# Layer 4's last twelve pairs of feature-major units with a Strassen scheme: seven products of quarters in place of eight

## Chip, cores and metric
One core of one Trainium2 chip. The time is device microseconds of one launch, the median of repeated runs. TensorE (PE in the profile) does the matrix products, VectorE (DVE) and ScalarE (ACT) the element work, SyncE (SP) issues the weight transfers. "PEld" is TensorE's loading of the stationary operand.

## What is computed
Two blocks of two layers each, in float32, on 512 tokens of 2048 features. Only layer 4 is touched by the change:

```python
u, v, z = jnp.split(h @ w_in, 3, axis=-1)          # h: 512 x 2048, w_in: 2048 x 6144
u = jax.nn.gelu(u)
v = layer_norm(jax.nn.gelu(v), ln_g, ln_b)
v = v.reshape(b, s // 128, 128, 8, 256)
mixed = jnp.einsum('gts,bnsgc->bntgc', w_s, v) + b_s.T[None, None, :, :, None]
y = u * mixed.reshape(b, s, 2048) * jax.nn.silu(z)
return y @ w_out
```

## The kernel before
Every product keeps float32 accuracy by splitting both operands into a high and a low part: `mm3` issues three matmuls (high x high, high x low, low x high) where a plain product has one. The layer's operand stands in SBUF as `Ah` and `Al`, 16 blocks of 128 features ("k blocks"), each 512 tokens wide. A weight chunk of 128 x 1024 is loaded into a `raw` tile by SP (`w_load`), copied to its high part `h` by ACT (`w_high`, L150) and subtracted to its low part `l` by DVE (`w_low`, L156); `w_get` keeps the preparation two chunks ahead of the chunk that it hands out, with four `h` and four `l` buffers and three `raw` buffers.

The program is unrolled by hand: each engine executes its own instructions in the order in which the code writes them. Element work that goes beside the products is written as generators in `self.side`; `pump`, called after every fourth k block of a unit (12 matmuls), lets each of them write its next piece. So the place of a piece among the matmuls is a count of pumps. `run_until` pumps with no matmul between until a condition holds.

Layer 4 first computes v, token-major, in four items (`tm_item`). Then 16 pairs of feature-major units (`fm_unit`): one of 128 features of u, one of 128 features of z, each 16 k blocks x 3 matmuls of 512 columns into one PSUM bank, two weight chunks. Beside the first units runs the generator `spatial` (from L1515): sums of squares on ACT; a layer norm on DVE (L1548 and L1549, 16 pairs of instructions, and some small ones for each of four token tiles; a `yield` after each pair); then 18 steps, each with the split of one column block of v (ACT cast L174, DVE subtraction L175), twelve small matmuls of 128 columns for the block split one pump before, and the bias addition L1556 for the one before that. Gelu of u is L1576, its product with the mixed v L1579; the tanh, sum and product for z are L937, L938 and L1589. After the 16 pairs the out projection (`out_proj`) begins: it multiplies with 512 columns (`fg_item`) and at its end with 256 (`fg_last`).

Of the kernel before, what the change touches and what calls it, by code (L numbers as in the profile page):

```python
# [6 lines left out]
F32 = mybir.dt.float32  # L7
# [3 lines left out]
ALU = mybir.AluOpType  # L11
# [5 lines left out]
KC = 16  # L17
# [10 lines left out]
SCH_END = ["", "S", "", "P", "c", "c", "c", "c"]  # L28


class Core:
# [76 lines left out]
    def w_ahead(self, n, dma=0):  # L108
        n = min(n, len(self.wlist))
        while self.wprep < n or self.wdma < dma:  # L110
            while self.wdma < max(dma, min(self.wprep + 3, len(self.wlist)) if self.wprep < n else 0):
# [17 lines left out]

    def w_load(self):  # L130
        raw = self.p_raw.tile([128, 1024], F32, tag="raw", name="raw")
        src = self.wlist[self.wdma]
        n = src.shape[1]
# [8 lines left out]
    def w_high(self):  # L142
        if self.wpend or self.wprep >= len(self.wlist):
            return
        while self.wdma < min(self.wprep + 3, len(self.wlist)):
            self.w_load()
        raw, n = self.wraw.pop(self.wprep)
# [19 lines left out]
    def mm3(self, out, lh, ll, rh, rl, start, stop):  # L167
        mm = self.nc.tensor.matmul
        mm(out=out, lhsT=lh, rhs=rh, start=start, stop=False)  # L169
        mm(out=out, lhsT=lh, rhs=rl, start=False, stop=False)  # L170
        mm(out=out, lhsT=ll, rhs=rh, start=False, stop=stop)  # L171
# [116 lines left out]
    def fg_last(self, kperm, bd):  # L288
        """The last two units, token half by token half."""
# [64 lines left out]
    # -- start: x from the input; 1/rms is applied to the first layer's products  # L354
# [67 lines left out]
    # during a layer's last products: the mix that is done takes the place of operands that nothing reads any more  # L422
# [15 lines left out]
    # -- out projection of a layer, feature by feature: B gets x_new * gain, xd[i] the residual stream  # L438
# [189 lines left out]
    # ---------------- layer 1  # L628
# [7 lines left out]
    def layer1(self):  # L636
# [25 lines left out]
        # log sigmoid of lambda, times 4, and half biases  # L662
# [311 lines left out]
    # ---------------- layer 2  # L974
# [307 lines left out]
    # ---------------- modulation rows  # L1282
# [57 lines left out]
    # ---------------- layer 3  # L1340
# [150 lines left out]
    # ---------------- layer 4  # L1491
    def plan4(self):
        a = self.a
        w = [a["w4t"][j, c] for j in range(4) for c in range(8)]
        w += [a["w4f"][u, c] for u in range(32) for c in range(2)]
        w += [a["wo4"][j, c] for j in range(4) for c in range(8)]
        return w

    def layer4(self):
# [3 lines left out]
        done = {}  # L1503
# [11 lines left out]
        def spatial():  # L1515
# [27 lines left out]
            for t in range(NT):  # L1543
                s = sums[t]
                r = self.rms_tile(s[:, 8:12])
                for j in range(4):
# [3 lines left out]
                    yield  # L1550
            X, P = {}, {}
            for i in range(KC + 2):
                if i >= 2:
# [4 lines left out]
                    done["s", m] = True  # L1558
                if 1 <= i <= KC:
# [38 lines left out]
        for n in range(KC):  # L1598
            self.fm_unit(evac_u(n))
            if n == KC - 1:  # L1600
                self.mix_early(list(range(KC)), lambda k: k in mix_done)
            self.fm_unit(evac_z(n))
        return list(range(KC)), lambda k: k in mix_done

    # ---------------- whole
    def run(self):
        L = self.layers
        plans = {1: self.plan1, 2: self.plan2, 3: self.plan3, 4: self.plan4}
        for l in L:
            self.wlist += plans[l]()  # L1610
# [49 lines left out]
def fm(w):  # L1660
    U = w.shape[1] // 128
    w = w.reshape(2, 8, 128, U, 128)
    return np.ascontiguousarray(w.transpose(3, 0, 2, 1, 4)).reshape(U, 2, 128, 1024)

# [16 lines left out]
def layout(inp):  # L1681
# [36 lines left out]
    # layer 2  # L1718
# [15 lines left out]
    # layer 3  # L1734
# [16 lines left out]
    # layer 4  # L1751
# [5 lines left out]
    d["w4f"] = fm(w[:, np.concatenate(order)])  # L1757
# [25 lines left out]
```

## Time and profile before
| what | value |
|---|---|
| median of three runs | 3379.75 us (3377.02 to 3380.16) |
| profiled execution, first to last instruction (its span, the only time listed of it) | 3376.1 us |
| TensorE busy | 3354.3 us, 99% of the span |
| VectorE, ScalarE busy | 1894.8 us (56%), 1223.4 us (36%) |
| TensorE's share of the chain that ended last | 99% |

The span leaves out what lies around the instructions, 3.65 us against the median. Busy shares are means over stages; layer 4 runs from about 2630 to the end, its 16 pairs of units from about 2802 to 3170.

### The profile page before, as it was taken

The numbers are of one execution on the slowest core, as the hardware profiler recorded it, in microseconds if no ns is written. First come the engines' busy times: TensorE is split into PE (matmuls) and PEld (weight loads), VectorE is DVE, ScalarE is ACT, GpSimd is POOL, SyncE is SP. The second block draws the span as 40 slices with busy tenths as digits, with TensorE's granted clock in tenths as the row PEclk, the third lists the DMA queues.
The fourth block names the chain that finished last, engine by engine and source line by source line (L and its number), as shares of the span: only waits on it lengthen the run. The fifth ranks groups of instructions, "written<-read, shape, count | busy, mean of one in ns | idle before, by whom it ended". The sixth has DMA issues, their size and how long they took to land.

```text
span 3376.1 us, 40334 instructions
## 1 busy us (share of the span) xinstructions
PE 3354.3 (99%) x15596; PEld 2766.4 (82%) x15596; DVE 1894.8 (56%) x3179; ACT 1223.4 (36%) x1966; POOL 113.5 (3%) x208
## 2 busy tenths in 40 slices
PE   9999999999999999999999999999999999999998
PEld 7888888888888888888888888888888888888887
DVE  7766676568656566564576665544434526533334
ACT  5355553343333233344542322322333424222332
POOL 0000000100000000001000000000000000000000
PEclk9999999999999999999999999999999999999999
DMA  5422235645454445444344444322333422223232
GB/s 207 153 81 81 76 103 182 202 133 173 153 162 152 157 153 179 136 156 145 123 141 156 149 161 171 109 88 88 112 125 129 144 96 88 97 97 107 95 107 92
DMA packets 155088, 443.92 MB, mean 131 GB/s; under 512 B 19429, under 2 KB 19557, under 8 KB 154896
## 3 DMA queue, kind: packets, MB, share of 16 engines
q1 hardware_dynamic: 140832, 398.95, 35.5%
q0 software_dynamic: 14064, 42.40, 4.0%
q8 instruction: 122, 2.00, 0.2%
q14 instruction: 70, 0.57, 0.1%
HBM read 424.36 MB, written 16.91 MB: 131 GB/s over the span
## 4 chain that ended last, share of the span: by engine, by line
PE 99%; DVE 0%; DMA 0%; ACT 0%; issue 0%; SPq 0%; DVEq 0%; ACTq 0%
PE ps L169 32%; PE ps L171 32%; PE ps L170 32%; PE ps L178 2%; DMA raw<-in_w1t 0%; PE ps L1310 0%; PE ps L1311 0%; PE ps L519 0%; DVE s L529 0%; PE ps L505 0%; DVE l L156 0%; SPq L366 0%; ACT h L150 0%; ACT B L484 0%; ACT s L479 0%
## 5 line engine op out<-in xcount | busy, mean ns | idle before, releaser
L169 PE MATMUL ps<-Ah,h 128*128 128x512 f32 (+1 forms) x3200 | 1240.2, 388 | 0.0
L171 PE MATMUL ps<-Ah,l 128*128 128x512 f32 (+1 forms) x3200 | 1230.1, 384 | 0.0
L170 PE MATMUL ps<-Al,h 128*128 128x512 f32 (+1 forms) x3200 | 1225.2, 383 | 0.0
L156 DVE TENSOR_TENSOR l<-raw,h 128x1024 fp32r<-128x1024 f32 (+2 forms) x559 | 675.0, 1209 | 735.4 <-ACT h L150 726.5
L150 ACT CAST h<-raw 128x1024 fp32r<-128x1024 f32 (+2 forms) x559 | 577.3, 1035 | 863.2 <-PE ps L170 503.0
L171 PEld LDWEIGHTS ps<-Ah,l 128*128 128x128 f32 x3200 | 601.7, 188 | 127.9
L170 PEld LDWEIGHTS ps<-Al,h 128*128 128x128 f32 x3200 | 602.1, 188 | 122.8 <-issue 0.2
L169 PEld LDWEIGHTS ps<-Ah,h 128*128 128x128 f32 x3200 | 602.3, 188 | 117.4 <-issue 0.2
L169 PE MATMUL ps<-h,Ah 128*128 128x512 f32 (+2 forms) x1408 | 547.9, 389 | 7.1 <-ACT h L174 5.8
L170 PE MATMUL ps<-l,Ah 128*128 128x512 f32 (+2 forms) x1408 | 543.9, 386 | 0.8 <-DVE l L156 0.8
L171 PE MATMUL ps<-h,Al 128*128 128x512 f32 (+2 forms) x1408 | 544.2, 386 | 0.4
L169 PEld LDWEIGHTS ps<-h,Ah 128*128 128x128 f32 x1408 | 265.5, 189 | 64.1 <-ACT h L174 5.8
L171 PEld LDWEIGHTS ps<-h,Al 128*128 128x128 f32 x1408 | 265.2, 188 | 60.9 <-DVE Al L551 1.6
L170 PEld LDWEIGHTS ps<-l,Ah 128*128 128x128 f32 x1408 | 265.4, 189 | 57.9 <-DVE l L156 1.1
L1301 DVE SCALAR_TENSOR_TENSOR s<-s,sc 128x512 f32<-128x512 f32 x360 | 268.8, 747 | 5.8 <-DMA s<-in_ab_wm 1.7
L175 DVE TENSOR_TENSOR s<-ps,s 128x512 fp32r<-128x512 f32 (+2 forms) x178 | 101.1, 569 | 153.8 <-ACT s L174 153.7
L174 ACT CAST s<-ps 128x512 fp32r<-128x512 f32 (+2 forms) x178 | 86.1, 491 | 242.9 <-PE ps L178 168.1
L169 PE MATMUL ps<-s 128*128 128x512 f32 (+2 forms) x384 | 131.6, 343 | 0.0
L171 PE MATMUL ps<-s 128*128 128x512 f32 (+2 forms) x384 | 129.5, 337 | 1.3 <-DVE s L175 1.3
L170 PE MATMUL ps<-s 128*128 128x512 f32 (+2 forms) x384 | 128.8, 335 | 0.0
L476 ACT ACTIVATE s<-s 128x512 f32<-128x512 f32 (+1 forms) x72 | 42.0, 583 | 136.3 <-DVE s L468 73.3
L171 PEld LDWEIGHTS ps<-s 128*128 128x128 f32 x384 | 72.5, 189 | 10.2 <-DVE s L175 1.5
(271 smaller groups left out, 2026.6 us busy)
## 6 DMA issues: line engine op xcount, KB each, us to landing
raw<-in_wo SPq DMA_DIRECT2D x128, 512.0 KB, 3.5
raw<-in_w3f SPq DMA_DIRECT2D x112, 512.0 KB, 3.5
s<-in_ab_wm SPq DMA_DIRECT2D x192, 256.0 KB, 4.2
s<-in_sg_wm SPq DMA_DIRECT2D x192, 256.0 KB, 4.1
raw<-in_w2t SPq DMA_DIRECT2D x88, 512.0 KB, 3.6
raw<-in_w4f SPq DMA_DIRECT2D x64, 512.0 KB, 3.5
raw<-in_w1f SPq DMA_DIRECT2D x48, 512.0 KB, 3.6
raw<-in_w2f SPq DMA_DIRECT2D x32, 512.0 KB, 3.6
```

Of the source, the lines that this page charges most:

```text
L150: self.nc.scalar.copy(out=h[:, 0:n], in_=raw[:, 0:n])
L156: self.nc.vector.tensor_tensor(out=l[:, 0:n], in0=raw[:, 0:n], in1=h[:, 0:n].bitcast(F32), op=ALU.subtract)
L169: mm(out=out, lhsT=lh, rhs=rh, start=start, stop=False)
L170: mm(out=out, lhsT=lh, rhs=rl, start=False, stop=False)
L171: mm(out=out, lhsT=ll, rhs=rh, start=False, stop=stop)
L174: self.nc.scalar.copy(out=h, in_=src)
L175: self.nc.vector.tensor_tensor(out=l, in0=src, in1=h.bitcast(F32), op=ALU.subtract)
L178: self.nc.tensor.transpose(out, src, self.idt)
L476: nc.scalar.activation(out=sq[0], in_=xn, func=AF.Square)
L1301: nc.vector.scalar_tensor_tensor(out=acc, in0=raw, scalar=ck, in1=acc, op0=ALU.mult, op1=ALU.add)
```

## The change
Of the 16 pairs of units in layer 4 the first `N4` = 4 stay as they are. The other 12 become `pair_unit`: u and z of a pair, times two token halves of 256, over k blocks 0 to 5 against 8 to 13 (`M4` = 6) are a 2 x 2 by 2 x 2 product of quarters, done with seven products instead of eight. The k blocks 6, 7, 14 and 15 are added in the ordinary way. Every matmul of a pair then has 256 columns: 7 products x 6 blocks x 3, and 2 features x 4 blocks x 2 halves x 3.

The weight sums are made on the fly: of eight chunks in a pair (seven of 768 columns, one of 1024) five are loaded and four are, or replace, a difference made on DVE in the `raw` tile before the split (`w.comb`, L193). The operand sums are made once: `pair_prep` makes three sums ("1", "2", "4") in three pieces of two k blocks each and keeps their high and low parts in 18 `s` tiles; `pair_last` overwrites the second token half of blocks 0 to 5 of `Ah` and `Al` with a difference ("3"). `pair_prep` is let into its first piece by the end of the layer norm, into its second when v's blocks 0 to 7 are mixed, into its third when all 16 are. Products that are needed twice are copied out of PSUM by ACT between the products (L338, L341, L344, L351, L380) and added on DVE (L352, L377 to L379); the next product but one of a pair goes into the same PSUM half. The layer norm yields after two pairs of instructions instead of one. The pool `raw` has 4 buffers instead of 3, the pool `s` 26 instead of 28.

```diff
-        self.p_raw = pool(name="raw", bufs=3)
+        self.p_raw = pool(name="raw", bufs=4)
-        self.p_s = pool(name="s", bufs=28)
+        self.p_s = pool(name="s", bufs=26)
...
+def pair_steps(q, r, m):
+    st = {}
+    n = m * 128
+    w = [Step(q[0], n, st, "a"), Step(q[1], n, st, "b", ("b", "b", "a")), Step(None, n, st, None, ("b", "c", "b")),
+         Step(None, n, st, "c"), Step(None, n, st, None, ("a", "b", "a")), Step(q[3], n, st, "d"),
+         Step(None, n, st, None, ("b", "d", "b"))]
+    w[2].src, w[2].key = q[2], "c"
+    w[6:6] = [Step(x, x.shape[1]) for x in r]
+    return w
...
+        if w.comb:
+            raw, x, y = (w.st[c] for c in w.comb)
+            self.nc.vector.tensor_tensor(out=raw[:, 0:n], in0=x[:, 0:n], in1=y[:, 0:n], op=ALU.subtract)
...
+    def pair_prep(self, m):
+        def raw(hf, k):
+            x = self.s()
+            tt(out=v(x), in0=q(self.Ah.bitcast(F32), hf, k), in1=q(self.Al.bitcast(F32), hf, k), op=ALU.add)
+            return x
+        def keep(nm, c, x):
+            h, l = self.sr(), self.sr()
+            self.split(h, l, x)
+            S[nm, c] = v(h), v(l)
+        for c in range(n):
+            while not self.pair_room(c):
+                yield
+            k = 2 * c
+            x21, x22 = raw(1, k), raw(1, 8 + k)
+            tt(out=x22, in0=x21, in1=x22, op=ALU.add)
+            yield
+            keep("1", c, x22)
+            x11 = raw(0, k)
+            tt(out=x22, in0=x22, in1=x11, op=ALU.subtract)
+            yield
+            keep("2", c, x22)
+            x12 = raw(0, 8 + k)
+            tt(out=x12, in0=x12, in1=x22, op=ALU.subtract)
+            yield
+            keep("4", c, x12)
...
+    def pair_last(self, m):
+        for c in range(m // 2):
+            k = 2 * c
+            x, y = self.s(), self.s()
+            for o, hf in ((x, 0), (y, 1)):
+                tt(out=v(o), in0=q(self.Ah.bitcast(F32), hf, k), in1=q(self.Al.bitcast(F32), hf, k), op=ALU.add)
+            tt(out=x, in0=x, in1=y, op=ALU.subtract)
+            self.split(q(self.Ah, 1, k), q(self.Al, 1, k), v(x))
+            yield
+        self.S["3"] = True
...
+    def pair_unit(self, m, evu, evv, early=()):
...
+        prod(x, A(lo, 0), True)
+        nc.scalar.copy(out=tu[:, lo], in_=x)
+        self.pump()
+        prod(y, S("1"), True)
+        nc.scalar.copy(out=t5[:, lo], in_=y)
+        self.pump()
+        prod(x, S("2"), False)
+        nc.scalar.copy(out=tv[:, lo], in_=x)
+        self.pump()
+        prod(y, S("4"), False)
+        self.pump()
+        if "3" not in self.S:
+            self.run_until(lambda: "3" in self.S)
+        prod(x, A(hi, 0), False)
+        nc.scalar.copy(out=tv[:, hi], in_=x)
+        nc.vector.tensor_tensor(out=tv[:, hi], in0=tv[:, hi], in1=t5[:, lo], op=ALU.add)
+        self.pump()
+        prod(w0, A(lo, 8), True)
...
+        prod(x, A(hi, 8), False)
...
@@ def layer4
-                    yield
+                    if j % 2:
+                        yield
+            done["ln"] = True
...
-        for n in range(KC):
+        self.pair_room = lambda c: ("ln" if c == 0 else ("sg", c - 1)) in done
+        self.S = None
+        self.add(self.pair_prep(M4))
+        for n in range(N4):
             self.fm_unit(evac_u(n))
-            self.fm_unit(evac_z(n))
+            self.fm_unit(evac_z(n))
+        self.run_until(lambda: self.S)
+        self.add(self.pair_last(M4))
+        for n in range(N4, KC):
...
+            self.pair_unit(M4, evac_u(n), evac_z(n), early)
```

How the instructions stand: first VectorE at the end of the layer norm, its last token tile. Before (L1548 and L1549 the norm, L156 the low part of a weight chunk, L175 the low part of v's first blocks):

```order
L1548 SCALAR_TENSOR_TENSOR B<-B,t,s 128x512
L1549 SCALAR_TENSOR_TENSOR B<-B,t,s 128x512
L156 TENSOR_TENSOR l<-raw,h 128x1024
L1548 SCALAR_TENSOR_TENSOR B<-B,t,s 128x512
L1549 SCALAR_TENSOR_TENSOR B<-B,t,s 128x512
L1548 SCALAR_TENSOR_TENSOR B<-B,t,s 128x512
L1549 SCALAR_TENSOR_TENSOR B<-B,t,s 128x512
L156 TENSOR_TENSOR l<-raw,h 128x1024
L1548 SCALAR_TENSOR_TENSOR B<-B,t,s 128x512
L1549 SCALAR_TENSOR_TENSOR B<-B,t,s 128x512
L175 TENSOR_TENSOR s<-B,s 128x512
```

and in the change (L1711 and L1712 the norm, L202 the weight chunk, L221 the low part of v's first block, L280 the first sums of `pair_prep`):

```order
L1711 SCALAR_TENSOR_TENSOR B<-B,t,s 128x512
L1712 SCALAR_TENSOR_TENSOR B<-B,t,s 128x512
L1711 SCALAR_TENSOR_TENSOR B<-B,t,s 128x512
L1712 SCALAR_TENSOR_TENSOR B<-B,t,s 128x512
L202 TENSOR_TENSOR l<-raw,h 128x1024
L1711 SCALAR_TENSOR_TENSOR B<-B,t,s 128x512
L1712 SCALAR_TENSOR_TENSOR B<-B,t,s 128x512
L1711 SCALAR_TENSOR_TENSOR B<-B,t,s 128x512
L1712 SCALAR_TENSOR_TENSOR B<-B,t,s 128x512
L221 TENSOR_TENSOR s<-B,s 128x512
L280 TENSOR_TENSOR s<-Ah,Al 128x512 x2
```

A token tile has one weight chunk among its norm instead of two. On TensorE the first small matmul of `spatial` stands behind 204 matmuls of the units instead of behind 300.

Second, VectorE in the change from the last bias additions of `spatial` (L1721), which stand at the start of the first pair's first product, on: the third piece of `pair_prep` (L280, L293, L297, L301 with the low parts L221), the z of unit 3 (L1099, L1756), the third weight chunk's difference and low part (L193, L202), and the first piece of `pair_last` (L315).

```order
L1721 TENSOR_TENSOR B<-ps,s 128x4x128 x2
L280 TENSOR_TENSOR s<-Ah,Al 128x512 x2
L293 TENSOR_TENSOR s<-s 128x512
L1099 SCALAR_TENSOR_TENSOR s<-s,ps 128x512
L1756 SCALAR_TENSOR_TENSOR B<-s,B 128x4x128
L221 TENSOR_TENSOR s<-s 128x512
L280 TENSOR_TENSOR s<-Ah,Al 128x512
L297 TENSOR_TENSOR s<-s 128x512
L221 TENSOR_TENSOR s<-s 128x512
L280 TENSOR_TENSOR s<-Ah,Al 128x512
L301 TENSOR_TENSOR s<-s 128x512
L221 TENSOR_TENSOR s<-s 128x512
```

None of this stands on VectorE before; there the units of pair 4 go on with one L156 in 24 matmuls. Third, ScalarE in the change over the same stretch (L220 the high parts, L196 the weights, L338 to L351 the copies out of PSUM):

```order
L220 CAST s<-s 128x512 x3
L196 CAST h<-raw 128x768
L338 COPY s<-ps 128x256
L220 CAST Ah<-s 128x2x256
L196 CAST h<-raw 128x768
L341 COPY s<-ps 128x256
L220 CAST Ah<-s 128x2x256
L196 CAST h<-raw 128x768
L344 COPY s<-ps 128x256
L220 CAST Ah<-s 128x2x256
L196 CAST h<-raw 128x768
L196 CAST h<-raw 128x1024
```

Each copy out of PSUM stands behind the cast of the weight chunk two products later.

## Rows read from the trace of the kernel before

**Rows 1.** The page: span, busy time of each engine, chain that ended last.
```profile
span 3376.1 us, 40334 instructions
...
PE 3354.3 (99%) x15596; PEld 2766.4 (82%) x15596; DVE 1894.8 (56%) x3179; ACT 1223.4 (36%) x1966; POOL 113.5 (3%) x208
...
PE 99%; DVE 0%; DMA 0%; ACT 0%; issue 0%; SPq 0%; DVEq 0%; ACTq 0%
```

**Rows 2.** Busy time by stretch: during the norm, and after `spatial`; columns in the first line.
```profile
core 0: us, PE busy (x) PEld busy (x) DVE busy (x) ACT busy (x) POOL busy (x), PEclk, DMA share, GB/s
...
2840.00:2852.00 12.00, 12.00 (x55) 9.82 (x54) 11.58 (x26) 2.63 (x4) 0.00 (x0) 1.00 0.26 87
...
2960.00:2972.00 12.00, 12.00 (x53) 9.70 (x52) 3.54 (x4) 2.58 (x3) 0.08 (x1) 1.00 0.34 110
```

**Rows 3.** Timeline of ScalarE: gelu of u (L1576), start us and us, 16 units apart.
```profile
2968.41 0.60 ACT L1576 ACTIVATE s<-ps 128x512 f32<-128x512 f32 x1 [4.78 <-PE ps L171]
...
3147.61 0.60 ACT L1576 ACTIVATE s<-ps 128x512 f32<-128x512 f32 x1 [4.78 <-PE ps L171]
```

**Rows 4.** Timeline of TensorE, 256 columns: layer 2's token-major item, and `fg_last`.
```profile
776.01 0.28 PE L169 MATMUL ps<-h,Ah 128*128 128x256 f32 x1
...
781.90 0.28 PE L170 MATMUL ps<-l,Ah 128*128 128x256 f32 x1
...
3337.80 0.28 PE L169 MATMUL ps<-Ah,h 128*128 128x256 f32 x1
...
3341.93 0.28 PE L171 MATMUL ps<-Ah,l 128*128 128x256 f32 x1
```

**Rows 5.** Groups by line: loads of the stationary operand; busy, mean ns of one.
```profile
L170 PEld LDWEIGHTS ps<-Al,h 128*128 128x128 f32 x3200 | 602.1, 188 | 122.8 <-issue 0.2
```

**Rows 6.** Timeline of VectorE: the norm's first and last, a chunk's low part, v's first split.
```profile
2824.88 0.74 DVE L1548 SCALAR_TENSOR_TENSOR B<-B,t,s 128x512 f32<-128x512 f32 x1
...
2829.24 1.23 DVE L156 TENSOR_TENSOR l<-raw,h 128x1024 fp32r<-128x1024 f32 x1 [2.84 <-ACT h L150]
...
2867.10 0.75 DVE L1549 SCALAR_TENSOR_TENSOR B<-B,t,s 128x512 f32<-128x512 f32 x1
2867.77 0.69 DVE L175 TENSOR_TENSOR s<-B,s 128x512 fp32r<-128x512 f32 x1
```

**Rows 7.** Timeline of TensorE: 22 matmuls of an early unit, first small matmul of `spatial`.
```profile
2808.03 0.39 PE L169 MATMUL ps<-Ah,h 128*128 128x512 f32 x1
...
2812.84 0.39 PE L169 MATMUL ps<-Ah,h 128*128 128x512 f32 x1
...
2871.20 0.22 PE L169 MATMUL ps<-s 128*128 128x128 f32 x1
```

**Rows 8.** Groups by line and form on VectorE and ScalarE; busy, mean ns of one.
```profile
L156 DVE TENSOR_TENSOR l<-raw,h 128x1024 fp32r<-128x1024 f32 x70 | 85.6, 1223 | 122.7 <-ACT h L150 122.7
...
L175 DVE TENSOR_TENSOR s<-B,s 128x512 fp32r<-128x512 f32 x16 | 10.9, 683 | 0.0
...
L489 DVE TENSOR_TENSOR s<-s 128x256 f32<-128x256 f32 x18 | 7.6, 424 | 4.1 <-ACT s L476 2.0 <-ACT s L481 1.7
...
L150 ACT CAST h<-raw 128x1024 fp32r<-128x1024 f32 x70 | 73.1, 1046 | 140.8 <-PE ps L170 109.3 <-PE ps L171 28.0 <-issue 3.6
...
L174 ACT CAST s<-B 128x512 fp32r<-128x512 f32 x16 | 9.6, 617 | 2.1 <-DVE B L1549 2.1
...
L1197 ACT COPY B<-ps 128x256 f32<-128x256 f32 x32 | 12.0, 374 | 89.0 <-PE ps L171 89.0
```

**Rows 9.** The page's transfers: KB each, us from issue to landing.
```profile
raw<-in_w4f SPq DMA_DIRECT2D x64, 512.0 KB, 3.5
```

**Rows 10.** The kernel's start: TensorE's timeline, and busy time 16 to 20 us.
```profile
17.06 0.62 PE L170 MATMUL ps<-l,Ah 128*128 128x512 f32 x1 [0.76 <-DVE l L156]
...
20.05 0.63 PE L171 MATMUL ps<-h,Al 128*128 128x512 f32 x1
...
20.47 0.50 PE L169 MATMUL ps<-h,Ah 128*128 128x512 f32 x1
...
16.00:20.00 4.00, 3.24 (x8) 2.30 (x8) 4.00 (x6) 4.00 (x7) 0.00 (x0) 0.66 1.05 398
```

More of the change, by code (lines that the diff above doesn't have):

```diff
@@ L128, in w_first, with w_plan, w_need @@
         self.wprep = 1
+    def w_plan(self, plan):
+        self.wloads = []
+        for x in plan:
+            w = x if isinstance(x, Step) else Step(x, x.shape[1])
+            if w.src is not None:
+                w.load = len(self.wloads)
+                self.wloads.append(w)
+            w.need = len(self.wloads)
+            self.wlist.append(w)
+    def w_need(self):
+        return min(self.wlist[self.wprep].need + 2, len(self.wloads))
     def w_load(self):
         raw = self.p_raw.tile([128, 1024], F32, tag="raw", name="raw")
-        src = self.wlist[self.wdma]
-        n = src.shape[1]
+        w = self.wloads[self.wdma]
+        n, src = w.n, w.src
         for p in self.w_parts(self.wdma):
@@ L144, in w_high @@
             return
-        while self.wdma < min(self.wprep + 3, len(self.wlist)):
+        while self.wdma < self.w_need():
             self.w_load()
-        raw, n = self.wraw.pop(self.wprep)
+        w = self.wlist[self.wprep]
+        n = w.n
+        if w.src is not None:
+            raw, _ = self.wraw.pop(w.load)
+            if w.st is not None:
+                w.st[w.key] = raw
+        elif w.key:
+            raw = w.st[w.key]
+        if w.comb:
+            raw, x, y = (w.st[c] for c in w.comb)
+            self.nc.vector.tensor_tensor(out=raw[:, 0:n], in0=x[:, 0:n], in1=y[:, 0:n], op=ALU.subtract)
         h = self.p_h.tile([128, 1024], F32R, tag="h", name="h")
@@ new lines, in pair_unit, with prod @@
+    def pair_unit(self, m, evu, evv, early=()):
+        nc = self.nc
+        X, Y, W = (self.ps() for _ in range(3))
+        lo, hi = slice(0, 256), slice(256, 512)
+        early = list(early)
+        A = lambda hf, k0: lambda j: (self.Ah[:, k0 + j, hf], self.Al[:, k0 + j, hf])
+        S = lambda nm: lambda j: tuple(x[:, j % 2] for x in self.S[nm, j // 2])
+        tu, tv, t5 = self.s(), self.s(), self.s()
+        def prod(out, get, start):
+            h, l = self.w_get()
+            for j in range(m):
+                ks = slice(j * 128, (j + 1) * 128)
+                self.mm3(out, h[:, ks], l[:, ks], *get(j), start and j == 0, j == m - 1, skip_group_check=True)
+        x, y, w0, w1 = X[:, lo], Y[:, lo], W[:, lo], W[:, hi]
+        prod(x, A(lo, 0), True)
[14 more added lines that the diff above has]
+        nc.vector.tensor_tensor(out=tv[:, hi], in0=tv[:, hi], in1=t5[:, lo], op=ALU.add)
+        self.pump()
+        prod(w0, A(lo, 8), True)
+        self.pump()
+        for _ in range(2):
+            if early:
+                early.pop(0)()
+        kr = list(range(m, 8)) + list(range(8 + m, 16))
+        nr = len(kr)
+        c = None
+        for u, outs in ((0, (w0, x)), (1, (y, w1))):
+            for i, k in enumerate(kr):
+                p = (u * nr + i) * 128
+                if p % 1024 == 0:
+                    c = self.w_get()
+                p %= 1024
+                for o, hf in zip(outs, (lo, hi)):
+                    self.mm3(o, c[0][:, p:p + 128], c[1][:, p:p + 128], self.Ah[:, k, hf], self.Al[:, k, hf], False,
+                             i == nr - 1, skip_group_check=True)
+            self.pump()
+            for _ in range(2):
+                if early:
+                    early.pop(0)()
+        prod(x, A(hi, 8), False)
+        tt = nc.vector.tensor_tensor
+        tt(out=tu[:, lo], in0=w0, in1=tu[:, lo], op=ALU.add)
+        tt(out=tv[:, hi], in0=w1, in1=tv[:, hi], op=ALU.add)
+        tt(out=tv[:, lo], in0=y, in1=tv[:, lo], op=ALU.add)
+        nc.scalar.copy(out=tu[:, hi], in_=x)
+        self.add(evu(tu))
+        self.add(evv(tv))
@@ L1494, in plan4 @@
         w = [a["w4t"][j, c] for j in range(4) for c in range(8)]
-        w += [a["w4f"][u, c] for u in range(32) for c in range(2)]
+        w += [a["w4f"][u, c] for u in range(2 * N4) for c in range(2)]
+        for n in range(KC - N4):
+            w += pair_steps(a["w4p"][n], [a["w4r"][n]], M4)
         w += [a["wo4"][j, c] for j in range(4) for c in range(8)]
@@ L1608, in run @@
         plans = {1: self.plan1, 2: self.plan2, 3: self.plan3, 4: self.plan4}
-        for l in L:
-            self.wlist += plans[l]()
+        self.w_plan([w for l in L for w in plans[l]()])
         dump = lambda l: dict(dump=l == L[-1])
@@ L1756, in layout @@
         order += [np.arange(128 * n, 128 * n + 128), np.arange(4096 + 128 * n, 4224 + 128 * n)]
-    d["w4f"] = fm(w[:, np.concatenate(order)])
+    d["w4f"] = fm(w[:, np.concatenate(order[:2 * N4])])
+    d["w4p"], d["w4r"] = fp(w[:, np.concatenate(order[2 * N4:])], M4)
     d["wo4"] = tmo(inp["sg_w_out_2"][0])
```

37 lines of the change are left out of this document (31 added, 6 removed).

## The prediction, before any run of the change
> **What bounds the kernel now.** I read the page's head first: TensorE is busy for 99% of the span and makes up 99% of the chain that ended last [rows 1]. So a product saved is time saved, as long as nothing makes TensorE wait where it does not wait now. The busy time by stretch then shows where that can happen: in the layer norm of layer 4 VectorE is busy 11.58 of 12 us, after `spatial` only 3.54 of 12, with TensorE at 12 of 12 in both [rows 2]. The change lays new VectorE work on both places. All sums are made against the profiled span, 3376.1 us, which lies 3.65 below the median of the runs, 3379.75; I add the same 3.65 at the end. 0.2%, about what a measurement can tell here from no change, is 6.8 us.
>
> **What the products save.** 16 units in a row take 3147.61 - 2968.41 = 179.20 us, so a unit takes 11.20, its 48 matmuls 0.2333 each, a pair 22.40 [rows 3]. A new pair has 7 x 6 x 3 = 126 matmuls in the products and 2 x 4 x 2 x 3 = 48 in the rest, 174 of 256 columns. Their step has two rows: 36 matmuls of `fg_last` from 3337.80 to 3341.93 give 4.13 / 35 = 0.118 us, layer 2's item 5.89 / 52 = 0.1133 [rows 4]. Half of 0.2333 is 0.1167: a short matmul costs a little more per column, or a little less. I take 0.118, because `fg_last` is like the new products in every operand: weights as the stationary operand, half rows of `Ah` and `Al` as the moving one. Then a pair takes 174 x 0.118 = 20.5 us, 1.9 less, and **12 pairs give -22.8**. At 0.1133 a pair takes 19.7 and they give -32.2; that is the other bound. The weight loads take 188 ns each [rows 5], longer than the step, yet `fg_last` keeps its step with them: they overlap.
>
> By the Trainium skill ("TensorE: Matmul & The Clock Gate", Back-to-back issue gap) an isolated step is columns / 2.4 plus 2.5 ns, an estimate of 215.8 and 109.2 ns here, and 12 pairs would give 12 x (96 x 0.2158 - 174 x 0.1092) = 20.6 us. Both measured steps of this kernel are longer, so the rows decide.
>
> **What the layer norm's place costs.** The norm yields half as often, so the first small matmul of `spatial` stands 96 matmuls earlier in TensorE's order. At this place a matmul steps 4.81 / 21 = 0.229 us [rows 7], so TensorE comes there 22.0 us earlier, at 2849.2 instead of 2871.20. It needs the low part of v's first block, and that stands on VectorE behind the whole norm: from 2824.88 to its end at 2867.8 VectorE has nearly no gap [rows 6]. Before, the low part is ready at 2867.77 + 0.69, that is 2.7 before TensorE asks. The norm itself is not made shorter. What leaves its stretch is four weight chunks (a 1.22 us instruction each [rows 8], some 1.13 back to back, 4.5), one sum of z (0.6), and some 1.4 of the wait of 2.84 for a cast [rows 6], which the second pair now fills: 6.5. So TensorE waits 22.0 - 2.7 - 6.5 = **+12.8**. The chunks that left are due only later; the bounds are 10 (if the whole 2.84 goes and other work slips behind) and 19.3 (if the norm ends where it did).
>
> After a wait TensorE comes back slow. In the kernel's start, behind waits of under 1 us, the granted clock of 16 to 20 us is 0.66, and from 17.06 to 20.05 seven steps take 0.427 us each, the lower level of 1.2 GHz; from 20.47 on it is 0.233 again [rows 10]. Eight such steps lose 8 x (0.427 - 0.233) = 1.6. I charge **+1.7** here. The Trainium skill's rule that speaks against this change is the same (the page above, HAM oscillation): a gap in TensorE's work returns the array to half rate, and the work behind it starts cold. By that rule a wait of 12.8 us costs about 14.5, and the rows of the start agree.
>
> **What the first pair costs.** Its second product needs the sums "1" of all three pieces. The third piece may start only when the 16th block of v is mixed, and that bias addition needs small matmuls that stand right ahead of the pair's first matmul. So let t = 0 be that matmul; products are due every 18 x 0.118 = 2.12. VectorE then has, in its order, nine instructions of 512 columns (addition, three for sum "1", two for z, a low part, two for sum "2"), some 0.65 each in a row (0.683 alone [rows 8]), to 6.0; a cast of 0.62; low part and two for sum "4", to 8.6; a cast, to 9.2; a low part, 9.9; the third chunk's difference at 768 columns (between 0.683 and 1.223, 0.95), 10.9; its cast (between 0.617 and 1.046, 0.83), 11.7. Only then stands the copy of the first product, 0.37 for 256 columns [rows 8]: 12.1. The third product writes the same PSUM half and was due at 4.24. It begins about 8 late, then waits 0.4 for the chunk's low part, to 12.9. From here `pair_last` runs through the same two engines: three pieces of two sums, a difference, a cast and a low part (3 x 0.65 + 0.62 + 0.65 = 3.2, three times 9.7), with the fourth chunk's low part (0.95) and the fifth's difference, cast and low part (2.7) between: 13.3, to 26.3. The fifth product's blocks 4 and 5 need the last piece and were due at 4 x 2.12 + 1.4 = 9.9. With semaphores I make it **+16.9**, and +1.0 for the clock (most of the slow steps lie beside waits that are counted). All of it is a chain of single instructions; the bounds are 13 (every instruction back to back, no hop) and 20.
>
> **What the other eleven pairs cost.** VectorE has per pair eleven instructions of 768 (0.87 in a row), one of 1024, four of 256 (0.424 [rows 8]) and three of 512: some 14.5 of 20.5 us. ScalarE has seven casts of 768, one of 1024, five copies, two activations: 10. Both fit, but in order: the fourth chunk's cast stands behind the copy of the first product, gelu and tanh; its low part ends near 6.2 where it is due at 6.6; the fifth's difference, cast and low part then end near 8.9 where they are due at 8.7. That is 0.2 a pair, **+2.2**; bounds 0 and 1 a pair. SP's transfers are of 384 to 512 KB, landing in 3.5 us [rows 9]; with four raw buffers the remaining chunk's transfer starts when the fourth's low part is made, lands near 9.8, and its low part near 12 is due at 12.9: no wait, with the smallest reserve of all. Past the change nothing new stands on POOL. `early` puts the same six splits into the last pair as before into the last unit: nothing. The smaller `s` pool can delay element work of layers 1 to 3, which TensorE's order covers; I take 0, bounds -2 and +4.
>
> **Sum.** -22.8 + 12.8 + 1.7 + 16.9 + 1.0 + 2.2 = **+11.8**: a span of 3387.9, a time of 3391.5.
>
> **The rivals.**
> First, the **short step**: 0.1133 instead of 0.118 in all pairs. Units do step either 0.229 or 0.233 in different stretches [rows 3, 7], so the faster state can hold. Then -32.2, the same waits, and the eleven pairs a bit tighter (+3): +3.2, a time of 3383, within 0.2%. It decides for "no change" once the mean step is under 0.1155. Against it: `fg_last`, which is most alike. Chance 0.25.
>
> Second, on the other side, **the first pair does not wait**: VectorE reaches the third piece's sums as fast as TensorE asks, so only the norm's place costs. For it: after `spatial` VectorE has 8 of 12 us free [rows 2]. Price, with the step at half of 0.2333 (12 x (22.40 - 174 x 0.1167) = 25.1): -25.1 + 14.5 + 2.2 = -8.4, a time of 3371.3; with the short step 3364. It decides for "faster" if the first pair costs less than about 1.6 us instead of 17.9, with the short step less than 8.7. Against it: the order itself, in which the addition that frees the third piece stands at the pair's start. Chance 0.20.
>
> Third, **every later pair waits**: if a product waits a microsecond each time for a chunk's low part or for a copy, the eleven pairs cost 11 to 15 instead of 2.2: 3402. The reserve of 0.4 and -0.2 us speaks for it, the free 6 us of VectorE per pair against it. Chance 0.07.
>
> Fourth, **the weight loads bind**: at 188 ns a step a pair would take 174 x 0.188 = 32.7, and twelve cost 124 us, 3515. `fg_last` has the same loads and steps 0.118 [rows 4, 5]. Chance 0.01. The Trainium skill (the page above, same section) says that in a stream the spacing is set by load and matmul both; no row here shows the load setting it.
>
> **How the numbers follow.** My sum keeps 0.47 (own range 3384 to 3399). All of it is slower by over 0.2%, but for its lowest part; with the third and fourth rival 0.50 for slower. The short step gives 0.25 and the edge of my own sum 0.03 to "within 0.2%": 0.28. The second rival gives 0.20 and the short step's lower tail 0.02 to "faster": 0.22. The range takes in the second rival with the short step below, 3364, and the third above, 3403.
>
> **What would show it.** In the changed profile: TensorE idle about 13 us near 2849, ended by VectorE's low part, and the granted clock down behind it; near 2925 a pair of 37 us instead of 20.5, its longest gap, about 7 us, before the third product, ended by ScalarE; then eleven pairs of 20.5 to 20.8 with a step of 0.118. Wrong would be: no gap at the norm (then the count of pumps misled me), a first pair under 25 us, or later pairs over 21.5.

## The result, and the profile after

| | median us | lowest to highest | profiled span |
|---|---|---|---|
| before, measured beside it | 3378.39 (4 runs) | 3376.02 to 3380.16 | 3376.1 |
| the change | 3397.04 (4 runs) | 3396.23 to 3398.12 | 3394.5 |

The change makes the kernel slower: ratio 1.0055, 95% interval 1.0041 to 1.0069, +18.7 us; the spans differ by 18.4. Forecast were 3391.5 us and +11.8.

The page's head after the change; it answers to [rows 1]:

```profile
span 3394.5 us, 42673 instructions
...
PE 3346.9 (99%) x16532; PEld 2805.9 (83%) x16532; DVE 2013.8 (59%) x3365; ACT 1279.2 (38%) x2086; POOL 113.4 (3%) x208
...
PE 96%; DVE 2%; ACT 1%; DMA 1%; issue 0%; SPq 0%; DVEq 0%; ACTq 0%
```

TensorE is busy 7.4 us less, but TensorE's share of the chain that ended last falls from 99% to 96%: the other 4% now run over VectorE, ScalarE and a transfer. The waits of TensorE from 2795 to 3215 us tell where (line waited for; us in total, times, longest):

```profile
PE ps L215 <- ACT s L338: 6.6, 1, 6.6
PE ps L217 <- DVE s L221: 4.7, 1, 4.7
PE ps L215 <- ACT s L220: 4.6, 1, 4.6
PE ps L217 <- DVE l L202: 3.0, 2, 2.2
PE ps L215 <- ACT s L344: 2.6, 1, 2.6
PE ps L215 <- ACT h L196: 1.8, 1, 1.8
PE ps L216 <- DVE s L221: 0.9, 1, 0.9
```

Their places, in TensorE's timeline (in brackets the idle time ahead of the instruction and what ended it):

```profile
2850.73 0.50 PE L217 MATMUL ps<-Ah,l 128*128 128x512 f32 x1 [2.20 <-DVE l L202]
2857.89 0.47 PE L215 MATMUL ps<-s 128*128 128x128 f32 x1 [4.59 <-ACT s L220]
2863.33 0.47 PE L217 MATMUL ps<-s 128*128 128x128 f32 x1 [4.75 <-DVE s L221]
...
2929.50 0.33 PE L215 MATMUL ps<-Ah,h 128*128 128x256 f32 x1
2934.29 0.38 PE L216 MATMUL ps<-s,h 128*128 128x256 f32 x1 [0.89 <-DVE s L221]
2941.78 0.58 PE L215 MATMUL ps<-s,h 128*128 128x256 f32 x1 [6.63 <-ACT s L338]
2952.12 0.58 PE L215 MATMUL ps<-Ah,h 128*128 128x256 f32 x1 [2.56 <-ACT s L344]
...
3192.39 0.39 PE L215 MATMUL ps<-Ah,h 128*128 128x256 f32 x1 [1.78 <-ACT h L196]
3193.65 0.39 PE L217 MATMUL ps<-Ah,l 128*128 128x256 f32 x1 [0.76 <-DVE l L202]
```

Three at the layer norm (11.5), three in the first new pair (10.1), two in the last (2.5). The last copy of a pair, L380 on ScalarE, marks the ends of the first, eleventh and twelfth:

```profile
2969.45 0.37 ACT L380 COPY s<-ps 128x256 f32<-128x256 f32 x1 [5.35 <-PE ps L217]
...
3177.61 0.37 ACT L380 COPY s<-ps 128x256 f32<-128x256 f32 x1 [2.42 <-PE ps L217]
3203.02 0.37 ACT L380 COPY s<-ps 128x256 f32<-128x256 f32 x1 [2.28 <-PE ps L217]
```

Pairs 2 to 11 take (3177.61 - 2969.45) / 10 = 20.82 each, the last 25.41, the first 39.95 from its first matmul at 2929.50 to its copy (about 21 in a steady pair). By stretch, from these rows and those of before:

| stretch | forecast | measured | how the measured one comes about |
|---|---|---|---|
| products, 12 pairs at the steady length, with the small waits in them | -20.6 | -19.0 | 12 x (20.82 - 22.40) |
| the layer norm's place | +14.5 | +15.9 | four plain pairs with `spatial`, first matmul to the next pair's first: 2803.95 to 2929.50, 125.6; before 109.7 (2802.52 to the out projection's first matmul at 3181.01, less twelve pairs of 22.40) |
| first pair | +17.9 | +18.9 | 39.95 against 21.0 |
| last pair | 0 | +4.6 | 25.41 - 20.82 |
| out projection to the end | 0 | -3.4 | its first matmul to the span's end: 191.7 (from 3202.82) against 195.1 (from 3181.01) |
| layers 1 to 3 and v | 0 | +1.4 | first gelu of u at 2815.15 against 2813.72 |
| sum | +11.8 | +18.4 | the difference of the spans |

### The profile page after: what moved, and what is told of

It reads as the page before. It is cut to its first block, busy times and chain, and to the rows that moved or that the text cites. A ratio compares the mean times of both kernels' runs of the same rounds, so it can differ in the third digit from the quotient of the medians.

```text
span 3394.5 us, 42673 instructions
## 1 busy us (share of the span) xinstructions
PE 3346.9 (99%) x16532; PEld 2805.9 (83%) x16532; DVE 2013.8 (59%) x3365; ACT 1279.2 (38%) x2086; POOL 113.4 (3%) x208
## 4 chain that ended last, share of the span: by engine, by line
PE 96%; DVE 2%; ACT 1%; DMA 1%; issue 0%; SPq 0%; DVEq 0%; ACTq 0%
PE ps L217 31%; PE ps L215 31%; PE ps L216 31%; PE ps L224 2%; DVE l L202 0%; DMA raw<-in_w1t 0%; DVE B L1711 0%; ACT s L1701 0%; DVE B L1712 0%; DMA raw<-in_w4r 0%; ACT h L196 0%; PE ps L1471 0%; PE ps L1472 0%; PE ps L680 0%; DVE s L690 0%
## 5 line engine op out<-in xcount | busy, mean ns | idle before, releaser
L215 PE MATMUL ps<-Ah,h 128*128 128x512 f32 (+1 forms) x3296 | 1224.1, 371 | 4.4 <-ACT s L344 2.6
L217 PE MATMUL ps<-Ah,l 128*128 128x512 f32 (+1 forms) x3296 | 1215.0, 369 | 3.0 <-DVE l L202 3.0
L216 PE MATMUL ps<-Al,h 128*128 128x512 f32 (+1 forms) x3296 | 1209.2, 367 | 0.1
L202 DVE TENSOR_TENSOR l<-raw,h 128x1024 fp32r<-128x1024 f32 (+2 forms) x607 | 709.9, 1172 | 720.3 <-ACT h L196 718.5
L196 ACT CAST h<-raw 128x1024 fp32r<-128x1024 f32 (+2 forms) x607 | 608.3, 1006 | 850.4 <-PE ps L216 394.1
L217 PEld LDWEIGHTS ps<-Ah,l 128*128 128x128 f32 x3296 | 621.9, 189 | 115.8 <-DVE l L202 3.8
L216 PEld LDWEIGHTS ps<-Al,h 128*128 128x128 f32 x3296 | 622.7, 189 | 105.4 <-DVE Al L221 0.4
L215 PEld LDWEIGHTS ps<-Ah,h 128*128 128x128 f32 x3296 | 622.6, 189 | 105.4 <-ACT s L344 2.8
L221 DVE TENSOR_TENSOR s<-ps,s 128x512 fp32r<-128x512 f32 (+2 forms) x178 | 100.9, 568 | 146.3 <-ACT s L220 146.1
L220 ACT CAST s<-ps 128x512 fp32r<-128x512 f32 (+2 forms) x178 | 86.1, 491 | 229.9 <-PE ps L224 153.8
L220 ACT CAST s<-s 128x512 fp32r<-128x512 f32 x67 | 40.6, 619 | 146.5 <-DVE s L1540 101.4
```

What stands on the lines that cost most here:

```text
L202: self.nc.vector.tensor_tensor(out=l[:, 0:n], in0=raw[:, 0:n], in1=h[:, 0:n].bitcast(F32), op=ALU.subtract)
L215: mm(out=out, lhsT=lh, rhs=rh, start=start, stop=False, **k)
L216: mm(out=out, lhsT=lh, rhs=rl, start=False, stop=False, **k)
L217: mm(out=out, lhsT=ll, rhs=rh, start=False, stop=stop, **k)
L220: self.nc.scalar.copy(out=h, in_=src)
L221: self.nc.vector.tensor_tensor(out=l, in0=src, in1=h.bitcast(F32), op=ALU.subtract)
```

## Experiments

Times are medians against the kernel before beside them (3377.1 to 3378.4). "First" is the first new pair from its first matmul to its last copy, "last" the last pair from copy to copy.

| run | us | ratio, 95% interval | first pair begins | first | last |
|---|---|---|---|---|---|
| the change | 3397.04 | 1.0055, 1.0041 to 1.0069 | 2929.50 | 39.95 | 25.41 |
| e8_half_norm | 3382.28 | 1.0013, 1.0003 to 1.0022 | 2915.79 | 39.52 | 25.32 |
| e1_yield_each | 3390.69 | 1.0038, 1.0025 to 1.0051 | 2926.19 | 36.83 | 26.59 |
| e2_n5 | 3391.49 | 1.0041, 1.0026 to 1.0056 | 2952.30 | 31.66 | 27.55 |
| e7_no_last | 3387.93 | 1.0030, 1.0019 to 1.0041 | 2929.47 | 31.85 | 23.16 |
| e9_no_last_fill | 3386.00 | 1.0024, 1.0015 to 1.0033 | 2929.42 | 29.41 | 25.16 |
| e4_xr_sync | 3388.98 | 1.0035, 1.0022 to 1.0048 | 2929.00 | 37.60 | 21.02 |
| e3_n6_yield_each | 3374.65 | 0.9990, 0.9980 to 1.0000 | 2960.28 | 28.98 | 24.75 |
| e5_n6_yield_xr | 3372.39 | 0.9982, 0.9973 to 0.9991 | 2957.93 | 31.60 | 20.82 |
| e6_n6_yield_xr_swap | 3372.57 | 0.9984, 0.9974 to 0.9993 | 2959.80 | 32.02 | 20.73 |
| e10_n6_yield_xr_fill | 3371.03 | 0.9981, 0.9972 to 0.9990 | 2959.46 | 31.79 | 20.81 |
| e11_n6_yield_xr_fill3 | 3369.33 | 0.9976, 0.9967 to 0.9985 | 2959.09 | 29.14 | 20.81 |

### The layer norm's place

Half of the norm's VectorE work left out:

```diff
-                    nc.vector.scalar_tensor_tensor(out=bj, in0=bj, scalar=r, in1=b4[j], op0=ALU.mult, op1=ALU.add)
```

> The changed kernel without the second of the norm's two VectorE instructions on each of the 16 blocks (the scale by the root mean square and the added offset are left out): 16 x 0.69 = 11.0 us less on VectorE between the rows at 2839 and 2867. Theory (VectorE's norm, now asked for 22 us earlier, makes TensorE wait): the three waits of 2.2, 4.6 and 4.8 fall to under 1.5 in all, the slow steps behind them go (about 4 us), and the time is 3381 to 3386. Rival (TensorE waits for the splits, a chain over ScalarE and VectorE that would be late whatever the norm takes): the waits keep 8 us or more, the time stays over 3392.

TensorE's waits before the first pair fell from 11.5 us to this one line:

```profile
PE ps L217 <- DVE s L221: 1.7, 2, 1.3
```

The first pair begins 13.7 us sooner, and the time is 14.8 lower: VectorE's norm is what TensorE waits for; with half of it gone the splits are hardly late. The two small waits come to 1.7, a little over the 1.5 expected.

The yield after each pair of instructions put back:

```diff
-                    if j % 2:
-                        yield
+                    yield
```

> One part undone: the layer norm yields after each pair of instructions again, so the first small matmul of spatial stands 96 matmuls later. Theory (TensorE waits for VectorE's chains): the waits of 2.2 + 4.6 + 4.8 us near 2850 to 2863 and the low clock behind them go, -13 to -15 us; but eight steps of spatial and the second piece of the sums now stand with no unit beside them ahead of the first pair, which gets 8 to 14 longer. Sum -6 to 0 against the changed kernel, 3391 to 3397. Rival (the norm's place costs nothing, the time goes into the step of the short matmuls): slower than the changed kernel by 8 or more, over 3405.

The waits at the norm are gone, yet the four plain pairs with `spatial` take 121.0 us (2805.15 to 2926.19), only 4.5 less. What remains of the cost has moved to the tail of `spatial` (first, its matmuls in TensorE's timeline, then the busy time by stretch; PEclk, the granted clock, stands behind the five engines):

```profile
2906.89 0.28 PE L216 MATMUL ps<-s 128*128 128x128 f32 x1
2910.06 0.48 PE L217 MATMUL ps<-s 128*128 128x128 f32 x1 [2.89 <-DVE s L221]
...
2926.19 0.52 PE L215 MATMUL ps<-Ah,h 128*128 128x256 f32 x1
```

```profile
2900.00:2907.00 7.00, 7.00 (x51) 6.47 (x50) 3.99 (x7) 1.11 (x2) 0.00 (x0) 1.00 0.00 0
...
2919.00:2922.00 3.00, 3.00 (x16) 3.00 (x15) 1.73 (x4) 0.00 (x0) 0.00 (x0) 0.50 0.00 0
```

With four plain pairs, `spatial` starts so late that their matmuls are used up before its 18 steps are. The rest run with nothing between: waits of 3.5, and then, at a granted clock of 0.50 (1.2 GHz), some 70 small matmuls at 0.213 instead of 0.111, some 7 us. So with four plain pairs it is a choice between a cost of 15.9 and one of 11.4.

One plain pair more, without the yield, and two more with it:

```diff
-N4 = 4
+N4 = 5
```

> One pair more stays as it was (5 of 16). Theory: the third piece of the sums is then made beside the last plain units, the waits before the second and third product of the first new pair (1.2 and 6.9 us) go, those for the overwritten half (sum 3) stay in part; first new pair near 28 to 30 us instead of 39.8; one pair less saved costs 1.6. Sum -8 to -10, 3387 to 3389. Rival (the first new pair is long because its matmuls run at the lower clock after the norm, or because of its own copies): the first new pair keeps 36 us or more, time 3397 or more.

3391.49, some 3 more than expected: the waits at the norm stayed, the wait of 6.6 for the third product is gone and the first pair fell from 39.95 to 31.66 (28 to 30 were expected), but the last pair rose by 2.1.

> 6 of 16 pairs stay as they were and the layer norm yields after each pair of instructions as before the change. Theory: no wait at the norm (-14), first new pair 28 to 30 us (-10), two pairs less saved (+3.2): about 3375, some 3 below the kernel before. Rival (new pairs cost as much as old ones whatever stands beside them): 3390 or more.

With two more plain pairs and the yield, TensorE has no wait before the first pair, and the small matmuls have units beside them to the end. Two pairs give up 2 x 1.58 of the saving for it; the time still falls by 22.4.

### The first pair

Without `pair_last`:

```diff
-        self.add(self.pair_last(M4))
+        self.S["3"] = True
```

> The changed kernel without pair_last: the first blocks of A12 - A11 are not made, so the fifth product uses A12 itself. In the changed kernel the first new pair takes 39.75 us, 18.9 more than a steady one (20.81). Theory of the prediction (the chain of pair_last sets the pair, slow steps cost 1): what is left is the wait of 0.9 and the wait of 6.6 before the third product, and about ten slow steps: 138 matmuls x 0.118 + 1 = 17.3 from 2941.8, a pair of 29.6 us, a time near 3387. Rival (the low clock behind the wait of 6.6 sets it, whatever pair_last does): some 20 us at a step of 0.213 stay, 94 x 0.095 = 8.9, a pair of 37.5 us, a time near 3395. Between: if only the stretch up to the second wait is slow (some 30 steps), 31.5 us and 3389.

The wait of 6.6 stays, and the pair takes 31.85: the value between the two theories. The stretches of this run:

```profile
2935.00:2941.80 6.80, 0.17 (x3) 0.04 (x1) 4.42 (x7) 2.43 (x5) 0.00 (x0) 0.71 0.00 0
2941.80:2948.00 6.20, 6.20 (x28) 5.98 (x29) 3.98 (x5) 3.44 (x6) 0.00 (x0) 0.50 0.41 110
2948.00:2961.00 13.00, 13.00 (x111) 13.00 (x111) 8.36 (x12) 3.12 (x5) 0.00 (x0) 1.00 0.34 111
```

So of the 18.9 us `pair_last`, with the slow steps behind its wait, is 8.1, and the other 10.8 are the late third product and the slow steps behind it. In the change itself the clock is low for longer: behind the second wait, 2.6 for the fifth product, it is at 0.50 once more, up to 2961.8:

```profile
2941.80:2946.00 4.20, 4.20 (x18) 3.96 (x18) 3.44 (x6) 1.59 (x3) 0.00 (x0) 0.50 0.00 0
2946.00:2952.00 6.00, 3.56 (x20) 3.04 (x18) 4.38 (x7) 1.69 (x4) 0.00 (x0) 0.78 0.33 90
...
2956.10:2961.80 5.70, 5.66 (x26) 5.66 (x27) 4.71 (x6) 2.88 (x4) 0.00 (x0) 0.50 0.37 119
```

The same kernel with 56 matmuls more, whose result nobody reads, where TensorE waits:

```diff
+        if not hasattr(self, "filled"):
+            self.filled = True
+            f = self.ps()
+            for j in range(56):
+                k = j % KC
+                nc.tensor.matmul(out=f[:, lo], lhsT=self.Ah[:, k, 0:128], rhs=self.Ah[:, k, lo], start=True, stop=True)
```

> As the run without pair_last (the same part left out), with 56 matmuls of 256 columns added between the first pair's second and third product, whose result nobody reads: 56 x 0.118 = 6.6 us, the length of the wait. If the wait alone costs, TensorE is no sooner at the end: the third product starts where it did, and the time is that of the run without pair_last, or up to 1 more. If the clock behind the wait costs, the added work keeps it up: the steps behind are 0.118, the third product starts within 0.3 us of where it did, the pair takes 28.6 to 29.5 us, and the time falls by what the slow steps cost: by 8.9 if they last 20 us, by 3 if 30 steps, by 1 if ten.

```profile
2935.00:2942.00 7.00, 7.00 (x59) 6.87 (x57) 4.61 (x7) 2.68 (x5) 0.00 (x0) 1.00 0.01 2
2942.00:2950.00 8.00, 7.78 (x65) 7.57 (x65) 6.01 (x8) 3.93 (x7) 0.00 (x0) 1.00 0.37 115
```

The third product starts where it did (2941.72 against 2941.76), nearly every step behind it is short, and the pair takes 2.44 us less with 56 matmuls more. The slow steps are a cost of their own, about 0.1 us each. In the whole time the gain does not stand out (the two intervals overlap): the last pair gives back 2.0. Its two waits are alike in both runs (1.3 and 0.8 without the fill, 1.6 and 0.8 with it), but 2 slow steps stand behind them in the one and 18 in the other. So a gain of 2 us in one pair of one execution could be chance; what speaks for the fill is that the granted clock stays at 1.00 through its whole first pair, here and in e11 below.

### The last pair

The chain of the change shows what the last pair waits for, and POOL's timeline what runs beside it:

```profile
3183.59 7.63 DMA raw<-in_w4r
3191.29 1.05 ACT h L196
3192.37 1.24 DVE l L202
```

```profile
3180.58 3.74 POOL L751 DMA_DIRECT2D s<-xd  x7 [10.81 <-PE ps L217]
3185.02 2.20 POOL L751 DMA_DIRECT2D s<-xd  x4 [0.70 <-PE ps L217]
```

The chunk's transfer, 512 KB, lands after 7.63 us where its median over the pairs 2 to 12 is 3.5. TensorE waits 2.5 for it and for what is made of it; the other 2.1 of the 4.6 are slow steps (16 matmuls in the 3 us from 3194, at a granted clock of 0.50). Eleven loads of 256 KB for the out projection's residual (L751) are issued in the same 7 us: they begin as the last pair's products have read the operand sums, whose `s` tiles then come free. Moved into SP's queue, behind the weight chunks:

```diff
-                nc.gpsimd.dma_start(out=x, in_=xsrc[4 * j + u])
+                (nc.sync if final else nc.gpsimd).dma_start(out=x, in_=xsrc[4 * j + u])
```

> The residual's loads of the last out projection go into SP's queue, behind the weights, instead of POOL's. Theory: in the last pair the remaining chunk's transfer took 7.6 us beside eleven such loads and kept TensorE waiting (last pair 25.4 us instead of 20.8); with the loads behind it the last pair takes 20.8 to 21.3: -4 to -4.6, 3392.5. Rival (the last pair is long because of the six early splits on VectorE and ScalarE): it stays at 25, time 3397.

The last pair took 21.02, as expected, and the transfer 5.05; in the other runs with the loads in POOL's queue (e1, e2, e3, e7, e8, e9) it took 6.97 to 8.51, in e5, e6, e10 and e11, with the loads in SP's, 3.5 to 3.6. The time fell by 8, not 4.5. Of the rest, 2.35 is the first pair, 0.5 its earlier start, and 0.65 the kernel before, which was that much faster beside this run. The first pair has the same waits of 0.9 and 6.6, then 3.1 where the change has 2.6, but the clock was back sooner: this stretch, where the change shows 0.50 throughout:

```profile
2956.00:2961.00 5.00, 5.00 (x44) 4.87 (x43) 4.05 (x6) 2.45 (x4) 0.00 (x0) 1.00 0.37 103
```

The two programs are the same up to this place, and neither issues one of these loads before 3169. So it shows how far one execution's low stretch can differ from another's behind like waits: 2 to 3 us in this pair.

### A version that beats both

e3 with the loads in SP's queue:

> Ten pairs instead of twelve, the norm yielding after each pair, and the last out projection's residual loads in SP's queue instead of POOL's. The run with ten pairs and that yield took 3374.65, its last pair 24.75 us. Here the last pair should take 20.8 to 21.0, as in the run of the changed kernel with the loads moved, and the first pair stay at 28.5 to 29: a time of 3370 to 3371, 0.2% under the kernel before. If the last pair's wait is not the loads' but the r chunk's own, nothing changes: 3374.5.

The last pair took 20.82, but of the 3.9 us gained there 2.6 went back in the first pair, by slow steps; the time fell by 2.3, to 3372.39, above the 3370 to 3371 expected. Then one product moved ahead of the one that waits for `pair_last`, in the first pair only:

```diff
+        if swap:
+            prod(w0, A(lo, 8), True)
+            self.pump()
         if "3" not in self.S:
...
-        prod(w0, A(lo, 8), True)
-        self.pump()
+        if not swap:
+            prod(w0, A(lo, 8), True)
+            self.pump()
```

> The run before with one thing more: in the first pair the product of blocks 8 to 13 of the lower half stands ahead of the product that needs pair_last (and their weight chunks in that order), so that TensorE has 2.1 us of work where it waits 3.2 for pair_last. If pair_last's chain sets the first pair's end, that product is taken out of what comes behind it: the pair is 2 us shorter, 3368 to 3369. If the chain is pushed back by the chunk's cast and low part that now come earlier (0.8 + 0.95), it keeps under 1 us of that: 3369.5 to 3371.

It kept nothing: 32.02 instead of 31.60. The waits of its first pair name the chunks' casts (L198 in this kernel's own lines) and the copy of the second product (L343):

```profile
PE ps L217 <- ACT h L198: 4.2, 2, 3.0
PE ps L217 <- ACT s L343: 1.7, 1, 1.7
```

The moved product needs a weight chunk sooner, and its cast and low part stand on the same two engines as `pair_last`. Then the fill, on e5:

```diff
+        if "3" not in self.S:
+            self.fill(15)
         prod(y, S("4"), False)
         self.pump()
+        if "3" not in self.S:
+            self.fill(25)
...
+    def fill(self, n):
+        f = self.ps()
+        for j in range(n):
+            k = j % KC
+            self.nc.tensor.matmul(out=f[:, 0:256], lhsT=self.Ah[:, k, 0:128], rhs=self.Ah[:, k, 0:256], start=True, stop=True)
```

> The run with ten pairs, the norm's yield after each pair and the residual loads in SP's queue (3372.39; first pair 31.6 us, in it waits of 1.7 and 2.5 and 37 steps of 0.213), with matmuls added in the first pair whose result nobody reads: 15 ahead of the fourth product and 25 behind it, 1.8 and 2.9 us, about the length of the two waits. If the clock behind the waits costs, the 37 steps fall to 0.118: 3.5 us less, a first pair of 28 to 28.5 us, 3368.5 to 3369.5. If it does not, or the added matmuls overshoot the waits, the time stays at 3372 or rises by up to 1.

`pair_last` had been issued when the second condition was read, so only the first 15 were there; the second wait grew to 3.2 and the first pair stayed at 31.79. With the condition read once, and a third fill of 20 inside the fifth product:

```diff
+        first = "3" not in self.S
+        if first:
+            self.fill(15)
...
+        if first:
+            self.fill(27)
...
-        prod(x, A(hi, 0), False)
+        prod(x, A(hi, 0), False, 20 if first else 0)
```

> In the run before, the 25 matmuls behind the fourth product were not issued: pair_last had been issued by then, so its waits stood where they were, and 34 slow steps stayed. Here three fills stand in the first pair whatever pair_last has issued: 15 matmuls ahead of the fourth product, 27 ahead of the fifth, 20 inside the fifth ahead of its fifth block, which reads the last piece of pair_last. If the clock behind the waits costs, the waits of 3.2 and 0.3 and the slow steps go: the fifth block starts where it did, 18.4 us into the pair, the 90 matmuls from there take 10.6, a first pair of 29.0 to 29.5 instead of 31.5, and 3368.5 to 3370. If the time is set by pair_last's chain alone, it stays at 3371 to 3372.

All that TensorE waits for from 2795 to 3215 us in this run, and one stretch of its first pair, where the run before shows 0.52:

```profile
PE ps L217 <- DVE l L202: 0.4, 2, 0.2
```

```profile
2978.00:2984.00 6.00, 6.00 (x55) 6.00 (x55) 5.04 (x7) 2.35 (x4) 0.00 (x0) 1.00 0.48 132
```

3369.33 us, 0.9976 of the kernel before (0.9967 to 0.9985), and under the change by 27.7. Against e5 the whole time falls by 3.1, of which 2.5 is the first pair. The intervals of the two overlap; that the waits and the slow steps of the first pair are gone is read from the rows.

## Why the prediction was right, and where it was off

**The products.** Forecast: 174 steps of 0.118 and 0.2 of waiting in each pair. The steps of the third pair, first over the three products of operand sums (54 steps from 2992.19 to 2998.65), then into the fifth product, then 35 steps in the fifth and sixth:

```profile
2998.77 0.28 PE L216 MATMUL ps<-Al,h 128*128 128x256 f32 x1
2998.99 0.39 PE L217 MATMUL ps<-Ah,l 128*128 128x256 f32 x1
2999.22 0.28 PE L215 MATMUL ps<-Ah,h 128*128 128x256 f32 x1
2999.81 0.28 PE L217 MATMUL ps<-Ah,l 128*128 128x256 f32 x1
...
3003.93 0.28 PE L216 MATMUL ps<-Al,h 128*128 128x256 f32 x1
```

Products of `Ah` and `Al` step (3003.93 - 2999.81) / 35 = 0.1177; the wait for the fifth chunk's low part, too short for the table of waits, is the two steps from 2998.77 to 2999.22, 0.21 too long, in each of the pairs 2 to 12: the +2.2 of the forecast, at its place. Products of the `s` tiles step 6.46 / 54 = 0.1196, and that was not in the sum: 54 x 0.0019, 0.1 a pair, 1.2 in all. The forecast took `fg_last` to be like the new products "in every operand"; three of the seven read `s` tiles, which `fg_last` does not. The short step did not come. By the Trainium skill ("TensorE: Matmul & The Clock Gate", Back-to-back issue gap) 256 columns would be an estimated 109.2 ns; no stretch of the new pairs shows it.

**The layer norm's place.** 12.8 of waiting and 1.7 for the clock were forecast, 11.5 and some 4 measured; that VectorE's chain is the cause, e8 shows. The wait is in three parts, since the first low part to be late is a weight chunk's and the low part of v's block comes after the cast, and behind each part the steps are slow.

**The first pair.** The third product was forecast "about 8 late"; it was due 4.24 after 2929.50 and came at 2941.78, 8.0 late. `pair_last` was forecast to end 26.3 after the pair's start. The chain of the change, from the bias addition to the last low part, with 30 rows between that have the order of the forecast:

```profile
2929.70 0.69 DVE B L1721
2930.39 1.21 DVE s L280 x2
...
2955.40 0.70 DVE Al L221
2956.14 0.58 PE ps L216
```

It ends at 26.6. The fifth product's blocks 4 and 5 were thus 16.7 late (forecast 16.9). The rest, 2.2, is the clock, forecast at 1.0: 26 steps of 0.213 up to 2961.8. That term was mis-sized; e9 and e11 show that it can be taken away. What the forecast took from [rows 10], that TensorE comes back slow after a wait, holds in each first pair here but those where the wait was filled. The Trainium skill's rule on it (the page above, HAM oscillation), that a gap returns the array to half rate, agrees: 0.50 in the rows above, though it does not show behind every short wait (1.00 in the last pair of e7).

**The last pair** is the step that failed, +4.6. The prediction called the remaining chunk's transfer the one "with the smallest reserve of all", took its landing as 3.5 [rows 9], and said that past the change nothing new stands on POOL. Nothing new does, but the old residual loads do, at another time: before, eight come between 2930 and 2960 and four one at a time between 3059 and 3094, here one at 3169 and eleven in a row from 3180.58. The first of the four, in POOL's timeline of the kernel before:

```profile
3059.63 0.54 POOL L590 DMA_DIRECT2D s<-xd  x1 [99.54 <-DVE B L1579]
```

That the residual loads are what the chunk's transfer waits beside, e4 shows; that the operand sums' `s` tiles hold them back until the last pair is read from the order of the two and was not tried with a larger pool.

**Behind the pairs.** The out projection ran 3.4 us faster, without a change in it. Its matmuls of 512 columns in the kernel before, then in the change, 38 steps from the first row to the second:

```profile
3229.77 0.40 PE L171 MATMUL ps<-Ah,l 128*128 128x512 f32 x1
...
3238.64 0.40 PE L170 MATMUL ps<-Al,h 128*128 128x512 f32 x1
```

```profile
3229.83 0.39 PE L216 MATMUL ps<-Al,h 128*128 128x512 f32 x1
...
3238.53 0.39 PE L215 MATMUL ps<-Ah,h 128*128 128x512 f32 x1
```

0.2334 and 0.2289; over its 672 such matmuls that is 3.0 of the 3.4. All eleven other kernels show 0.229 there too. The prediction had seen both steps and put nothing for a change between them. What sets which one a stretch has is open: in the kernel before and in the change alike it goes from 0.229 to 0.233 inside layer 4, once the small matmuls of `spatial` have begun (from 2871.20 and 2857.89); only the change is back at 0.229 behind its pairs of 256 columns.

**Layers 1 to 3** (+1.4): the first gelu of u comes between 2814.28 and 2817.04 in the twelve profiles of changed kernels, which nothing in them explains; the term is within that spread, and the smaller `s` pool was not tried by itself.

Of the rivals, "every later pair waits" and "the weight loads bind" did not come about; "the first pair does not wait" is excluded by the rows above. The price of the weight loads, 3515, is mis-added: it sets the 124 on top of the forecast's 3391.5, which already holds the -22.8 of the products; with the waits of the sum it would be 3538. The direction came out right by terms that were each within 2 us, but for the last pair and the out projection, which partly cancel: that the sum of the spans is off by 6.6 and not by 10 is luck.

## What to carry to other kernels

Seven products for eight saved 7% of a pair (1.58 of 22.40) where the columns fall by 9%: half as many columns step at slightly more than half the time, and every chunk's low part has half the time to be made. That is soon used up by the start: count what operand sums and their place cost the engines beside TensorE, and give that work plain units to run beside (here six plain pairs and the norm's earlier yield, not four pairs) before the new scheme begins. Where a wait of TensorE can't be removed, matmuls that nobody reads, about as long as the wait, cost nothing here and kept the clock up. A pool that holds tiles longer moves the transfers that wait for them, also those of a stage the change does not touch: look where they land, and beside which transfer with little reserve.

## What the runs showed of the hardware that was not expected

- The granted clock behind like waits came back at different times: in the change it is 0.50 from 2956.1 to 2961.8, in e4 1.00 from 2956 on, a first pair of 39.95 against 37.60. In the last pair of e7 it is 1.00 behind waits of 1.3 and 0.8, in that of e9 0.50 behind waits of 1.6 and 0.8.
- Matmuls of 512 columns at a granted clock of 1.00 step either 0.2289 or 0.2333 us over long stretches, and the out projection went from the one to the other in all twelve changed kernels, none of which changes its products; this is worth 3.0 us there.
- A transfer of 512 KB beside eleven of 256 KB on another queue took 7.63 us to land where 3.5 is the median; with these loads behind it in its own queue it took 5.05 in e4 and 3.5 to 3.6 in the four later runs.
